# Two wide products and a sum for each rotation of the SSM, and one scan over two pairs

## The chip, the cores and the metric

The kernel runs on one core of a Trainium2 chip. The metric is the time of one execution on the device in microseconds. Five engines work side by side, each through its own queue in order: PE (matmuls), DVE (VectorE), ACT (ScalarE), POOL (GpSimd) and SP (here only transfers).

## The reference

One decoder block of 256 tokens and a model width of 2048, in float32. Cut to what the change touches:

```python
u    = rms_norm(x); proj = u @ w_in           # q, k, v, s_in, two gates
y_a  = diff_attention(q, k, v)                # 8 heads
a_bar = exp(lam * dt); b_bar = (a_bar - 1) / lam * b      # 64 groups x 64 complex states
bu   = einsum('gph,lgh->lgp', b_bar, s_in)
states = associative_scan(s[l] = a_bar * s[l-1] + bu[l])  # over the 256 tokens
y_s  = real(einsum('ghp,lgp->lgh', c, states)) + d * s_in
y_s  = gelu(y_s); y_s = y_s * sigmoid(y_s @ w_glu + b_glu)
merged = sigmoid(g_a) * (y_a @ w_attn_branch) + sigmoid(g_s) * (y_s @ w_ssm_branch)
x = x + rms_norm(merged @ w_out); x = x + rms_norm(swiglu(rms_norm(x)))
```

The decay of a state, a_bar = r * exp(i w), is taken apart: bu is turned back by the angle w * n of its token n, the two real parts are scanned with the real decay r alone, and the result is turned forward again. Each turn, a rotation, is four products and two sums.

## The kernel before

All matmuls of the main stream work in float32 by a split of each 128 x 1024 piece of weights into `hi` (ACT casts) and `lo` (DVE subtracts), from `do_split`. One k step of a block is four pairs of token half and column half with three matmuls of 512 columns each, 12 in all. The blocks follow one another: `ssm` (the projection of s_in), `q`, `k`, `v`, `ga0`, `ga1` (16 k steps each), `wa0`, `wa1` (8 each), `gs0`, `gs1` (16 each), then `glu`, which needs the output of the SSM, `ws0` and so on, and the feed-forward layer. `hi` and `lo` have three buffers each, so they run two to three k steps ahead of PE.

The rest is laid beside that stream as tasks, Python generators: `prep()` (decays, angles, the tables of sines and cosines, the input matrices), `u_parts()`, `ssm()` and `attn()`. After each k step `pump()` runs the first task on until the units that it yields exceed a budget: 1.2 units for a k step of block `ssm`, `SIDE` = 1.4 for the blocks up to `gs1`. Debt is carried over. `post_u` puts `u_parts()` first and appends `ssm()`; `post_v`, at the end of `v`, appends `attn()` and sets "switch", at which `ssm()` goes behind `attn()` in the list at its next pass. `glu_pre` calls `drain("s5")`: what is left of `ssm()` is then issued at once.

`pump` unpins the order: the program is handed to a planner (`schedule_with_timeline_sim=True`), which orders each engine's instructions while it builds the program, by a timeline of its own, and may take later ones forward when their inputs and buffers are ready. Tiles are given out from pools with a number of buffers: `side2` (the `bu` products of the SSM, the attention's scores) has one, `b8` six of 8 KB per partition.

`ssm()` works in 16 half steps (`hh`), two for each of 8 groups, of 128 partitions x 2 pairs x 256 tokens. In each:

- `table(hh + 1)` makes the next tables on POOL, six operations of 512 columns into `tcs` and `tss` (two buffers each, tags tabC and tabS);
- in odd half steps `group(g + 1)` prepares the output matrices (`cdup` on ACT, two transposes, `blkC`);
- the first rotation on DVE: four products of `bu` in PSUM with the tables into tA to tD (tags ssA to ssD), two sums;
- `finish` of the group before (8 matmuls and an operation on DVE), then the `bu` matmuls of the next half step (`bu_mm`) and the fetch of the one after;
- four scans of 256 columns, two for each pair;
- the second rotation: four products and two sums into `sre` and `sim`.

Yields in a half step: 1.2 three times, 0.7 twice, 1.2 twice, and 0.3 for `group`, 0.4 for `finish`.

Of the kernel before, what the change touches and what calls it, by code (L numbers as in the profile page):

```python
# [9 lines left out]
F32 = mybir.dt.float32  # L10
# [4 lines left out]
ALU = mybir.AluOpType  # L15
# [3 lines left out]
P = 128  # L19
S = 256  # L20
# [3 lines left out]
NG = 8  # L24
# [64 lines left out]
def hybrid_block_kernel(  # L89
# [9 lines left out]
    V, A, T = (InOrder(tc, e, pin) for e in (nc.vector, nc.scalar, nc.tensor))  # L99
    G = nc.gpsimd  # L100
# [17 lines left out]
    mixp = phase.enter_context(tc.tile_pool(name="mixp", bufs=1))  # L118
# [52 lines left out]
    ga = gap.tile([P, 2, 2, 1024], F32, name="ga")  # L171
# [229 lines left out]
    hold = {}  # L401
# [76 lines left out]
    def prep():  # L478
# [2 lines left out]
        G.affine_select(out=maskb, in_=maskb, pattern=[[-1, P]], compare_op=ALU.is_ge,  # L481
                        fill=-1e30, base=0, channel_multiplier=1)
        fl = lambda t_: t_.rearrange("p a b -> p (a b)")
        pp = Scratch([ga.rearrange("p a b c -> p (a b c)"), fl(small([P, 4, S], "sre")), fl(small([P, 4, S], "sim"))])
        braw = [big8(shape=(32, 2048)) for _ in range(2)]
        for ap, r, n in rows:
            G.dma_start(prow[r:r + n, :], ap)
# [38 lines left out]
        rr = mixp.tile([P, 32], F32, name="rr")  # L526
# [10 lines left out]
        fl = lambda t_: t_.rearrange("p a b -> p (a b)")  # L537
# [22 lines left out]
        for t_ in braw:  # L560
# [3 lines left out]
                          t_.rearrange("a (q h) -> a h q", h=16)[:, h, :], 32)  # L564
            bps.append(ps.rearrange("p (h a) -> p h a", h=16))
            yield 0.5
        bb = [mixp.tile([P, 32, 16], F32, name=nm("bb")) for _ in range(2)]
        bc = lambda c_: c_.unsqueeze(1).broadcast_to([P, 16, 32])
        tmp = [pp.tile([P, 16, 32], F32, name=nm("bt")) for _ in range(2)]
        for o, (c0, c1, op) in enumerate(((cre, cim, ALU.subtract), (cim, cre, ALU.add))):  # L570
# [6 lines left out]
        for base in (0, 4):  # L577
# [6 lines left out]
            for l in range(4):  # L584
                n = 1 << l
# [10 lines left out]
        hold.update(bb=bb, tabs=tabs, cn=cn)  # L596
        blkB, blkC = [], []
        for i in range(2):
            blkB.append([mixp.tile([P, 4, 32], F32, name=nm("blkB")) for _ in range(2)])
            blkC.append([mixp.tile([P, 4, 32], F32, name=nm("blkC")) for _ in range(2)])  # L600
            for t_ in blkB[i] + blkC[i]:
                G.memset(t_, 0.0)
        hold.update(blkC=blkC)
        yield 0.1
# [22 lines left out]
    def table(hh):  # L627
        (cb, sb), (ca, sa) = hold["tabs"]
        sl = slice(2 * hh, 2 * hh + 2)
        tcs = small([P, 2, 16, 16], "tabC", bufs=2)  # L630
        tss = small([P, 2, 16, 16], "tabS", bufs=2)
        t2 = small([P, 2, 16, 16], "tabt2")
        lo = lambda t_: t_[:, sl, :].unsqueeze(2).broadcast_to([P, 2, 16, 16])
        hi = lambda t_: t_[:, sl, :].unsqueeze(3).broadcast_to([P, 2, 16, 16])
        G.tensor_tensor(tcs, hi(ca), lo(cb), op=ALU.mult)
        G.tensor_tensor(t2, hi(sa), lo(sb), op=ALU.mult)
        G.tensor_tensor(tcs, tcs, t2, op=ALU.subtract)
        G.tensor_tensor(tss, hi(sa), lo(cb), op=ALU.mult)  # L638
        G.tensor_tensor(t2, hi(ca), lo(sb), op=ALU.mult)
        G.tensor_tensor(tss, tss, t2, op=ALU.add)  # L640
        r = lambda t_: t_.rearrange("p j a b -> p j (a b)")
        return r(tcs), r(tss)

    def u_parts():

# [22 lines left out]
    def ssm():  # L668
        uT = hold["yT"]
        nxt = table(0)  # L670

        def finish(g, bC, sre, sim):
            yp = side()
            for o, st in enumerate((sre, sim)):
                for j in range(4):
                    T.matmul(yp[32 * j:32 * j + 32, :S], bC[o][:, j, :], st[:, j, :],
                             start=(o == 0), stop=(o == 1), skip_group_check=True)
            V.scalar_tensor_tensor(uT[:, g, :], uT[:, g, :], dT[:, g:g + 1], yp[:, :S],
                                   op0=ALU.mult, op1=ALU.add)
# [37 lines left out]
        pend = None  # L717
        yield from group(0)
        fetch(0)
        bu = bu_mm(0)  # L720
        fetch(1)
        yield 1.0
        for hh in range(2 * NG):
            g, hf = hh // 2, hh % 2
            if hf == 0:
                bC = hold["bC"]
                sre = sim = None
            tcs, tss = nxt
# [4 lines left out]
            tA, tB, tC, tD = (small([P, 2, S], "ss" + n) for n in "ABCD")  # L733
            prr, pii = bu[:, :, 0:S], bu[:, :, S:2 * S]
            V.tensor_tensor(tA, prr, tcs, op=ALU.mult)
            V.tensor_tensor(tB, pii, tss, op=ALU.mult)
            yield 1.2
            V.tensor_tensor(tA, tA, tB, op=ALU.add)
            V.tensor_tensor(tC, pii, tcs, op=ALU.mult)
            yield 1.2  # L740
            V.tensor_tensor(tD, prr, tss, op=ALU.mult)
            V.tensor_tensor(tC, tC, tD, op=ALU.subtract)
            yield 1.2
            if pend:
                finish(*pend)
                pend = None
                yield 0.4
            if hold.pop("switch", None):
                yield "switch"
            if hh + 1 < 2 * NG:  # L750
                bu = bu_mm(1 - hf)
                if hh + 2 < 2 * NG:
                    fetch(hh + 2)
            for jj in range(2):
                rb = hold["rr"][:, 2 * hh + jj:2 * hh + jj + 1].broadcast_to([P, S])
                V.tensor_tensor_scan(tB[:, jj, :], rb, tA[:, jj, :], 0.0, op0=ALU.mult, op1=ALU.add)
                V.tensor_tensor_scan(tD[:, jj, :], rb, tC[:, jj, :], 0.0, op0=ALU.mult, op1=ALU.add)
                yield 0.7
            if sre is None:
                sre = small([P, 4, S], "sre")  # L760
                sim = small([P, 4, S], "sim")
            V.tensor_tensor(tA, tB, tcs, op=ALU.mult)
            V.tensor_tensor(tC, tD, tss, op=ALU.mult)
            V.tensor_tensor(sre[:, 2 * hf:2 * hf + 2, :], tA, tC, op=ALU.subtract)
            yield 1.2
            V.tensor_tensor(tB, tB, tss, op=ALU.mult)
            V.tensor_tensor(tD, tD, tcs, op=ALU.mult)
            V.tensor_tensor(sim[:, 2 * hf:2 * hf + 2, :], tB, tD, op=ALU.add)
            yield 1.2
            if hf == 1:  # L770
                pend = (g, bC, sre, sim)
        yield 2.5
        finish(*pend)
        y1h, y1l = big8(F32R, (P, 8, S)), big8(F32R, (P, 8, S))
# [185 lines left out]
    def first_load(k, r):  # L960
# [464 lines left out]
```

## Time and profile before

| | |
|---|---|
| median of 3 runs | 1436.42 us (1436.34 to 1437.39) |
| the profiled execution | 1436.86 us |
| its span, first to last instruction | 1435.1 us |
| busy: PE, DVE, ACT, POOL | 1375.7, 923.2, 680.8, 232.9 us |
| granted TensorE clock, mean | 0.985 |

The page gives busy times of the engines over the span and in 40 slices of 35.9 us (a digit is the busy share in tenths); the other views cut the trace by stretch, by group of instructions and by tile. In the names `side` is a tile in PSUM for side work, `acc` an accumulator of the main stream, `b` a tile of the pool `b8`. POOL's spans are rough, and matmuls are pipelined, so that their busy times overlap.

### The profile page before, as it was taken

How to read it: one execution, taken by the hardware profiler on the slowest of the kernel's cores; microseconds unless marked ns; L12 is line 12 of the kernel's file. 1: busy time of each engine (PE TensorE's matmuls, PEld its weight loads, DVE VectorE, ACT ScalarE, POOL GpSimd, SP SyncE). 2: the span in 40 equal slices, each digit the busy share in tenths (PEclk: the TensorE clock that was granted, in tenths of full speed). 3: DMA queues.
4: the chain of work that ended last, by engine and by line, in shares of the span. 5: the costliest groups of instructions: out<-in, count | busy, mean ns of one | idle time of the engine just before them, and what ended most of it. 6: DMA issues, size and time to landing. Idle time of an engine off the chain costs nothing.

```text
span 1435.1 us, 17346 instructions
## 1 busy us (share of the span) xinstructions
PE 1375.7 (96%) x6367; PEld 1115.7 (78%) x6367; DVE 923.2 (64%) x1122; ACT 680.8 (47%) x989; POOL 232.9 (16%) x195
## 2 busy tenths in 40 slices
PE   8998898999899879999999999999999999999997
PEld 6887676668676659888788888888888888888885
DVE  5965999967999975754764444444444445555555
ACT  4654443497443354444464444444444435444443
POOL 3293545500645500000000000000000000000001
PEclk9999999999999999999999999999999999999999
DMA  8688555444456465655576555556565564555651
GB/s 259 187 263 253 171 175 154 141 132 140 154 158 176 145 184 207 227 197 191 188 238 202 197 182 196 176 191 205 176 199 185 175 211 171 204 200 182 205 176 59
DMA packets 102006, 266.70 MB, mean 186 GB/s; under 512 B 10176, under 2 KB 17168, under 8 KB 98528
## 3 DMA queue, kind: packets, MB, share of 16 engines
q1 hardware_dynamic: 100704, 260.09, 56.1%
q10 hardware_dynamic: 608, 4.20, 0.8%
q0 software_dynamic: 608, 1.30, 0.4%
q8 instruction: 50, 0.82, 0.2%
q14 instruction: 36, 0.29, 0.1%
HBM read 257.16 MB, written 8.39 MB: 185 GB/s over the span
## 4 chain that ended last, share of the span: by engine, by line
issue 55%; PE 23%; DVE 15%; ACT 3%; DMA 2%; SPq 1%; POOL 0%; POOLq 0%; DVEq 0%; ACTq 0%
PE acc L41 22%; DVE lo L41 4%; DVE ssA L41 2%; DVE ssB L41 2%; DVE ssD L41 2%; PE side L41 2%; DVE ssC L41 2%; DMA raw<-in_w_in_dram 1%; DVE sim L41 1%; ACT hi L41 1%; SPq L623 1%; DMA raw<-in_w_glu_dram 1%; ACT prob L41 1%; DVE sre L41 1%; DVE b L41 1%
## 5 line engine op out<-in xcount | busy, mean ns | idle before, releaser
L41 DVE TENSOR_TENSOR lo<-raw,hi 128x1024 fp32r<-128x1024 f32 (+1 forms) x341 | 439.7, 1294 | 246.5 <-ACT hi L41 243.0
L41 ACT CAST hi<-raw 128x1024 fp32r<-128x1024 f32 (+1 forms) x340 | 355.0, 1051 | 399.0 <-PE acc L41 316.8
L41 PE MATMUL acc<-lo,zT_h 128*128 128x512 f32 x704 | 275.1, 391 | 0.0
L41 PE MATMUL acc<-hi,zT_l 128*128 128x512 f32 x704 | 274.3, 390 | 0.0
L41 PE MATMUL acc<-hi,zT_h 128*128 128x512 f32 x704 | 271.2, 393 | 0.2 <-ACT zT_h L41 0.2
L41 DVE TENSOR_TENSOR lo<-b,hi 128x1024 fp32r<-128x1024 f32 x124 | 151.1, 1224 | 147.6 <-ACT hi L41 147.6
L41 PE MATMUL acc<-lo,xT_h 128*128 128x512 f32 x512 | 207.4, 408 | 14.1 <-DVE lo L41 14.1
L41 PE MATMUL acc<-hi,xT_l 128*128 128x512 f32 x512 | 202.0, 397 | 0.0
L41 ACT CAST hi<-b 128x1024 fp32r<-128x1024 f32 x124 | 130.6, 1053 | 120.4 <-PE acc L41 104.0
L41 PE MATMUL acc<-hi,xT_h 128*128 128x512 f32 x512 | 165.8, 407 | 5.8 <-ACT hi L41 4.1
L41 PEld LDWEIGHTS acc<-hi,zT_h 128*128 128x128 f32 x704 | 132.3, 188 | 27.6 <-ACT zT_h L41 0.7
L41 PEld LDWEIGHTS acc<-hi,zT_l 128*128 128x128 f32 x704 | 132.3, 188 | 27.6
L41 PEld LDWEIGHTS acc<-lo,zT_h 128*128 128x128 f32 x704 | 132.3, 188 | 26.5
L41 PEld LDWEIGHTS acc<-lo,xT_h 128*128 128x128 f32 x512 | 98.8, 193 | 44.2 <-DVE lo L41 22.4
L41 PEld LDWEIGHTS acc<-hi,xT_h 128*128 128x128 f32 x512 | 97.6, 194 | 29.2 <-ACT hi L41 5.1
L41 PEld LDWEIGHTS acc<-hi,xT_l 128*128 128x128 f32 x512 | 98.3, 192 | 20.1 <-issue 0.8
L398 POOL TENSOR_TENSOR rstdf<-rstdfm,half 128x1 f32<-128x1 f32 x2 | 1.1, 546 | 691.6 <-DVE rstdfm L41 691.6
L41 PE MATMUL acc<-hi,b 128*128 128x512 f32 x256 | 84.1, 403 | 1.3 <-DVE ga L41 1.0
L638 POOL TENSOR_TENSOR tabS<-tabs,tabc 128x512 f32<-128x512 f32 x16 | 46.9, 2932 | 143.9 <-DVE ssB L41 143.9
L41 PE MATMUL acc<-lo,hTh 128*128 128x512 f32 x176 | 68.5, 389 | 0.0
L41 PE MATMUL side<-lo,hTh 128*128 128x512 f32 x176 | 68.5, 389 | 0.0
L41 PE MATMUL side<-hi,hTh 128*128 128x512 f32 x176 | 68.5, 389 | 0.0
(209 smaller groups left out, 1796.0 us busy)
## 6 DMA issues: line engine op xcount, KB each, us to landing
raw<-in_w_in_dram SPq DMA_DIRECT2D x127, 512.0 KB, 3.9
raw<-in_w_ffn_gate_dram SPq DMA_DIRECT2D x96, 256.0 KB, 2.8
raw<-in_w_ffn_up_dram SPq DMA_DIRECT2D x96, 256.0 KB, 3.1
raw<-in_w_ffn_down_dram SPq DMA_DIRECT2D x44, 512.0 KB, 3.7
b<-in_w_ffn_down_dram SPq DMA_DIRECT2D x22, 1024.0 KB, 4.9
b<-in_w_ffn_gate_dram SPq DMA_DIRECT2D x40, 512.0 KB, 3.8
b<-in_w_ffn_up_dram SPq DMA_DIRECT2D x40, 512.0 KB, 4.7
raw<-in_w_out_dram SPq DMA_DIRECT2D x32, 512.0 KB, 4.1
```

Of the source, the lines that this page charges most:

```text
L41: ins = f(*a, **kw)
L398: G.tensor_tensor(r, ms, half[:, :n], op=ALU.pow)
L623: nc.sync.dma_start(stack_b[:, j // 2, n, :, j % 2].rearrange("g q o n -> q g o n"), t_[32 * j:32 * j + 32])
L638: G.tensor_tensor(tss, hi(sa), lo(cb), op=ALU.mult)
```

## The change

The tables of a half step become one tile of three planes, minus sine, cosine and sine (`tab`); POOL makes the last two, ACT the first by `A.mul` with -1. A rotation is then a product of the real part with planes 0 and 1, one of the imaginary part with planes 1 and 2, each of 1024 columns with the part read twice by a broadcast, and a sum of 1024. The scans of both pairs are one of 512 columns for the real and one for the imaginary part; so that the second pair starts afresh, the decay is a tile of 512 columns with a zero at the start of each pair, which POOL fills for each half step (`decays`). `sre` and `sim` become one tile `st`, tA to tD become X and Y. `bb` and `blkB` move from their own tiles into one of the six buffers of `b8`. The yields become 1.3 three times, 1.2 twice, 1.3 three times.

```diff
-        bb = [mixp.tile([P, 32, 16], F32, name=nm("bb")) for _ in range(2)]
+        tmp8 = big8()
+        bb = [tmp8[:, 512 * i:512 * i + 512].rearrange("p (a h) -> p a h", a=32) for i in range(2)]
...
+        decay = mixp.tile([P, 2, S], F32, name="decay")
+        G.memset(decay[:, :, 0:1], 0.0)
...
     def table(hh):
-        tcs = small([P, 2, 16, 16], "tabC", bufs=2)
-        tss = small([P, 2, 16, 16], "tabS", bufs=2)
+        tab = small([P, 3, 2, S], "tab", bufs=2)
+        tcs, tss = (tab[:, i].rearrange("p j (a b) -> p j a b", a=16) for i in (1, 2))
...
+    def decays(hh):
+        d = hold["decay"]
+        G.tensor_copy(d[:, :, 1:S], hold["rr"][:, 2 * hh:2 * hh + 2].unsqueeze(2).broadcast_to([P, 2, S - 1]))
...
         nxt = table(0)
+        decays(0)
+        A.mul(nxt[:, 0], nxt[:, 2], -1.0)
...
-            V.tensor_tensor(tA, prr, tcs, op=ALU.mult)
-            V.tensor_tensor(tB, pii, tss, op=ALU.mult)
-            yield 1.2
-            V.tensor_tensor(tA, tA, tB, op=ALU.add)
-            V.tensor_tensor(tC, pii, tcs, op=ALU.mult)
-            yield 1.2
-            V.tensor_tensor(tD, prr, tss, op=ALU.mult)
-            V.tensor_tensor(tC, tC, tD, op=ALU.subtract)
-            yield 1.2
+            X, Y = (small([P, 2, 2, S], "ss" + n) for n in "XY")
+            both = lambda v: v.unsqueeze(1).broadcast_to([P, 2, 2, S])
+            V.tensor_tensor(X, both(bu[:, :, 0:S]), tab[:, 0:2], op=ALU.mult)
+            yield 1.3
+            V.tensor_tensor(Y, both(bu[:, :, S:2 * S]), tab[:, 1:3], op=ALU.mult)
+            yield 1.3
+            V.tensor_tensor(X, X, Y, op=ALU.add)
+            yield 1.3
...
-            for jj in range(2):
-                rb = hold["rr"][:, 2 * hh + jj:2 * hh + jj + 1].broadcast_to([P, S])
-                V.tensor_tensor_scan(tB[:, jj, :], rb, tA[:, jj, :], 0.0, op0=ALU.mult, op1=ALU.add)
-                V.tensor_tensor_scan(tD[:, jj, :], rb, tC[:, jj, :], 0.0, op0=ALU.mult, op1=ALU.add)
-                yield 0.7
...
+            for o in range(2):
+                V.tensor_tensor_scan(fl(Y[:, o]), fl(hold["decay"]), fl(X[:, o]), 0.0, op0=ALU.mult, op1=ALU.add)
+                yield 1.2
+            if hh + 1 < 2 * NG:
+                decays(hh + 1)
...
+            V.tensor_tensor(sh, both(Y[:, 1]), tab[:, 1:3], op=ALU.mult)
+            yield 1.3
+            V.tensor_tensor(X, both(Y[:, 0]), tab[:, 0:2], op=ALU.mult)
+            yield 1.3
+            if hh + 1 < 2 * NG:
+                A.mul(nxt[:, 0], nxt[:, 2], -1.0)
+            V.tensor_tensor(sh, sh, X, op=ALU.add)
+            yield 1.3
```

## Rows read from the trace of the kernel before

**Rows 1.** The page: the busy share of PE and DVE, 40 slices, in tenths.
```profile
PE   8998898999899879999999999999999999999997
...
DVE  5965999967999975754764444444444445555555
```
**Rows 2.** Table by stretches of instructions on tile acc alone (us; busy and count by engine).
```profile
251.00:345.60 94.60, 71.27 (x287) 51.97 (x285) 0.74 (x1) 2.04 (x3) 1.00 0.45 138
345.60:523.90 178.30, 149.05 (x598) 110.86 (x597) 5.88 (x9) 4.27 (x7) 0.98 0.53 161
```
**Rows 3.** The chain that ended last: a stretch of undisturbed matmuls (start us, us).
```profile
617.85 72.79 PE acc L41 x321
```
**Rows 4.** The table by stretches of all instructions: PE, PEld, DVE, ACT, POOL, clock.
```profile
140.50:251.00 110.50, 100.40 (x446) 76.71 (x445) 110.40 (x130) 46.86 (x64) 57.17 (x31) 0.95 0.56 169
251.00:345.60 94.60, 88.66 (x481) 67.87 (x480) 70.37 (x120) 64.22 (x161) 24.37 (x18) 1.00 0.45 138
345.60:523.90 178.30, 162.09 (x748) 121.81 (x746) 177.12 (x221) 81.30 (x126) 79.81 (x44) 0.98 0.53 161
```
**Rows 5.** Timelines of DVE, PE and ACT at the SSM's marks (start us, duration us).
```profile
251.07 0.68 DVE L41 TENSOR_TENSOR ssA<-side,tabC 128x512 f32<-128x512 f32 x1
...
345.61 0.64 PE L41 MATMUL side<-us,bs 96*128 96x256 f32 x4
...
519.89 0.68 DVE L41 TENSOR_TENSOR sim<-ssB,ssD 128x512 f32<-128x512 f32 x1
...
523.49 0.39 PE L41 MATMUL acc<-hi,xT_l 128*128 128x512 f32 x1
...
526.54 1.99 ACT L41 CAST hi<-raw 128x1024 fp32r<-128x1024 f32 x2 [5.85 <-DMA raw<-in_w_glu_dram]
...
532.24 0.80 PE L41 MATMUL acc<-b,hi 128*128 128x256 f32 x2 [8.37 <-ACT b L41]
```
**Rows 6.** Timeline of DVE late in gs1, POOL idle: starts and durations.
```profile
501.21 1.21 DVE L41 TENSOR_TENSOR lo<-raw,hi 128x1024 fp32r<-128x1024 f32 x1
502.34 0.68 DVE L41 TENSOR_TENSOR sre<-ssA,ssC 128x512 f32<-128x512 f32 x1
502.94 0.68 DVE L41 TENSOR_TENSOR ssD<-ssD,tabC 128x512 f32<-128x512 f32 x1
...
511.15 1.26 DVE L41 TENSOR_TENSOR_SCAN ssB<-rr,ssA 128x256 f32<-128x256 f32 x2
512.33 1.24 DVE L41 TENSOR_TENSOR_SCAN ssD<-rr,ssC 128x256 f32<-128x256 f32 x2
```
**Rows 7.** Groups of DVE instructions, 345.6 to 523.9 us: busy us, mean ns.
```profile
L41 DVE TENSOR_TENSOR lo<-raw,hi 128x1024 fp32r<-128x1024 f32 x50 | 70.1, 1408 | 0.0
L41 DVE TENSOR_TENSOR ssA<-ssA,ssB 128x512 f32<-128x512 f32 x9 | 10.0, 1116 | 0.0
L41 DVE TENSOR_TENSOR sim<-ssB,ssD 128x512 f32<-128x512 f32 x9 | 9.8, 1089 | 0.0
L41 DVE TENSOR_TENSOR ssC<-ssC,ssD 128x512 f32<-128x512 f32 x9 | 8.7, 967 | 0.0
L41 DVE TENSOR_TENSOR ssB<-side,tabS 128x512 f32<-128x512 f32 x9 | 6.1, 677 | 0.0
```
**Rows 8.** Groups over the whole span: a product with a broadcast operand.
```profile
L41 DVE TENSOR_TENSOR ga<-side,par 128x512 f32<-128x512 f32 x8 | 5.5, 687 | 3.7 <-PE side L41 3.7
```
**Rows 9.** Tile tabS and tabt: the shortest and longest table operations (min/median/max ns).
```profile
L639 POOL TENSOR_TENSOR tabt<-tabc,tabs x16: 1053/1061/2144, 108.3 to 488.9; 128x512 f32<-128x512 f32 x16
L638 POOL TENSOR_TENSOR tabS<-tabs,tabc x16: 1442/3178/4313, 102.8 to 482.0; 128x512 f32<-128x512 f32 x16
```
**Rows 10.** Tile qk: first and last start of the score matmuls, duration of a copy.
```profile
L41 PE MATMUL side<-qk x64: 272/374/379, 259.9 to 336.8; 64*128 64x128 f32 x32, 64*128 64x256 f32 x32
L41 ACT COPY qk<-side x8: 567/586/597, 231.6 to 330.2; 128x512 f32<-128x512 f32 x8
```
**Rows 11.** Tile cdup: first and last start of the copies.
```profile
L41 ACT COPY cdup<-cn x16: 292/299/311, 24.3 to 427.7; 128x128 f32<-128x128 f32 x16
```

More of the change, by code (lines that the diff above doesn't have):

```diff
@@ L483, in prep @@
         fl = lambda t_: t_.rearrange("p a b -> p (a b)")
-        pp = Scratch([ga.rearrange("p a b c -> p (a b c)"), fl(small([P, 4, S], "sre")), fl(small([P, 4, S], "sim"))])
+        pp = Scratch([ga.rearrange("p a b c -> p (a b c)"), small([P, 2 * 4 * S], "st")])
         braw = [big8(shape=(32, 2048)) for _ in range(2)]
@@ L598, in prep @@
         for i in range(2):
-            blkB.append([mixp.tile([P, 4, 32], F32, name=nm("blkB")) for _ in range(2)])
+            blkB.append([tmp8[:, c:c + 128].rearrange("p (a b) -> p a b", a=4)
+                         for c in (1024 + 256 * i, 1152 + 256 * i)])
             blkC.append([mixp.tile([P, 4, 32], F32, name=nm("blkC")) for _ in range(2)])
@@ L603, in prep @@
         hold.update(blkC=blkC)
+        decay = mixp.tile([P, 2, S], F32, name="decay")
+        G.memset(decay[:, :, 0:1], 0.0)
+        hold["decay"] = decay
         yield 0.1
@@ L640, in table @@
         G.tensor_tensor(tss, tss, t2, op=ALU.add)
-        r = lambda t_: t_.rearrange("p j a b -> p j (a b)")
-        return r(tcs), r(tss)
+        return tab
+    def decays(hh):
+        d = hold["decay"]
+        G.tensor_copy(d[:, :, 1:S], hold["rr"][:, 2 * hh:2 * hh + 2].unsqueeze(2).broadcast_to([P, 2, S - 1]))
     def u_parts():
@@ L670, in ssm, with finish @@
         nxt = table(0)
-        def finish(g, bC, sre, sim):
+        decays(0)
+        A.mul(nxt[:, 0], nxt[:, 2], -1.0)
+        def finish(g, bC, st):
             yp = side()
-            for o, st in enumerate((sre, sim)):
+            for o in range(2):
                 for j in range(4):
-                    T.matmul(yp[32 * j:32 * j + 32, :S], bC[o][:, j, :], st[:, j, :],
+                    T.matmul(yp[32 * j:32 * j + 32, :S], bC[o][:, j, :], st[:, o, j, :],
                              start=(o == 0), stop=(o == 1), skip_group_check=True)
@@ L726, in ssm @@
                 bC = hold["bC"]
-                sre = sim = None
-            tcs, tss = nxt
+                st = None
+            tab = nxt
             if hh + 1 < 2 * NG:
@@ L732, in ssm @@
                 yield from group(g + 1)
-            tA, tB, tC, tD = (small([P, 2, S], "ss" + n) for n in "ABCD")
-            prr, pii = bu[:, :, 0:S], bu[:, :, S:2 * S]
-            V.tensor_tensor(tA, prr, tcs, op=ALU.mult)
-            V.tensor_tensor(tB, pii, tss, op=ALU.mult)
-            yield 1.2
-            V.tensor_tensor(tA, tA, tB, op=ALU.add)
-            V.tensor_tensor(tC, pii, tcs, op=ALU.mult)
-            yield 1.2
-            V.tensor_tensor(tD, prr, tss, op=ALU.mult)
-            V.tensor_tensor(tC, tC, tD, op=ALU.subtract)
-            yield 1.2
+            X, Y = (small([P, 2, 2, S], "ss" + n) for n in "XY")
[6 more added lines that the diff above has]
+            yield 1.3
             if pend:
@@ L753, in ssm @@
                     fetch(hh + 2)
-            for jj in range(2):
-                rb = hold["rr"][:, 2 * hh + jj:2 * hh + jj + 1].broadcast_to([P, S])
-                V.tensor_tensor_scan(tB[:, jj, :], rb, tA[:, jj, :], 0.0, op0=ALU.mult, op1=ALU.add)
-                V.tensor_tensor_scan(tD[:, jj, :], rb, tC[:, jj, :], 0.0, op0=ALU.mult, op1=ALU.add)
-                yield 0.7
[L759 to L769, printed above, removed]
+            fl = lambda v: v.rearrange("p j n -> p (j n)")
+            for o in range(2):
+                V.tensor_tensor_scan(fl(Y[:, o]), fl(hold["decay"]), fl(X[:, o]), 0.0, op0=ALU.mult, op1=ALU.add)
+                yield 1.2
+            if hh + 1 < 2 * NG:
+                decays(hh + 1)
+            if st is None:
+                st = small([P, 2, 4, S], "st")
+            sh = st[:, :, 2 * hf:2 * hf + 2, :]
+            V.tensor_tensor(sh, both(Y[:, 1]), tab[:, 1:3], op=ALU.mult)
[6 more added lines that the diff above has]
+            yield 1.3
             if hf == 1:
-                pend = (g, bC, sre, sim)
+                pend = (g, bC, st)
         yield 2.5
```

## Prediction

> **What bounds the kernel now.** I read the page first. PE is nearly full in every slice but those between some 100 and 530 us, and there DVE is at its fullest [rows 1]. The time to be won or lost lies there: where PE is undisturbed, 321 accumulating matmuls take 72.79 us, 0.227 us each [rows 3]. I then cut the table by stretches at the SSM's own marks [rows 4]: the first six half steps of `ssm()` (140.5 to 251 us), the attention (to 345.6), the last nine half steps (to 523.9), the wait in front of `glu`. In the first DVE is busy for 110.4 of 110.5 us, in the third for 177.1 of 178.3: there DVE sets the pace and PE waits for `lo`. In the second DVE has 24 us to spare. At the end PE stands still for 8.4 us until the last gelu and cast are through [rows 5].
>
> A k step of the main stream (12 matmuls) needs 12 x 0.227 = 2.72 us of PE. The attention's stretch holds 287 of these matmuls, 24 k steps at 4.0 us, the third 598, 50 k steps at 3.6 [rows 2]: PE could do them in 2.72 each and the little work beside.
>
> **Part by part: the arithmetic on DVE.** Removed from each of 16 half steps: twelve products and sums of 512 columns and four scans of 256. Start to start an undisturbed 512 takes 0.60 us and a scan 0.59 (1.18 for two) [rows 6]: 12 x 0.60 + 4 x 0.59 = 9.56 us. Added: six of 1024 columns and two scans of 512. The 1024 columns of `lo` take 1.13 start to start [rows 6], so about 0.07 us per instruction is fixed. The new products read a broadcast operand and two of them PSUM; PSUM costs a product nothing now (677 ns [rows 7]), and a broadcast operand 687 [rows 8]. I take 1.13, and for a scan of 512 the two old ones less one fixed part, 1.11 (bounds 0.59 and 1.18). 6 x 1.13 + 2 x 1.11 = 9.0 us. Gain 0.55 us a half step, at most 8.8 us over 16.
>
> Beside POOL, DVE is slower: in the third stretch three of the four sums average 1116, 967 and 1089 ns against 677, 1.1 us a half step, and 50 `lo` average 1408 against 1210, another 1.1 [rows 6, 7]. POOL's six table operations (1.05 to 1.44 us at their shortest, up to 4.31 [rows 9]) stay and start at the same point, after the last read of the older table. POOL gets one more, the copy of the decays, for which the trace has no like: between 0.3 and 1.4 us. If a seventh operation disturbs as the six do, it costs DVE 0.4 us, if it falls on products from PSUM nothing; I take 0.25. Net gain on DVE: 0.3 us a half step, 5 us in all (bounds 2 and 8.8).
>
> `A.mul`, the minus sine plane, adds 16 ACT operations of 512 columns, 0.6 us each like `qk` (0.59 [rows 10]); ACT is busy for 81 of 178 us [rows 4], so I put it at nothing. But it waits for POOL in ACT's queue, with the `hi` casts and evacuations behind it; that is a rival below. `bb` and `blkB` in a `b8` buffer and the zeros of `decay` lie in `prep()`; I put them at nothing, since `u`'s buffer is free by then. Should the buffer be late, the first rotation (140.5 us) moves back with it, a few us.
>
> **Part by part: how the work is handed out.** This is the term that decides. A half step yields 7.4 units now (1.2 x 3 + 0.7 x 2 + 1.2 x 2) and 10.2 after (1.3 x 3 + 1.2 x 2 + 1.3 x 3), though it is no longer on DVE. Each k step of the main stream still releases 1.4. `prep()` and `u_parts()` need 37 units, of which the `ssm` block pays 16 x 1.2, so they end near k step 13 of `q`. From there to `glu` are 116 k steps, 162 units. Before, the attention (28.8), sixteen half steps (118), `group` and `finish` (5) and start and tail (8) ask for 160: it fits. After, they ask for 205. Followed k step by k step, twelve half steps and the thirteenth's scans are handed out in front of `glu`, and half steps 13, 14 and 15 (counted from 0) come only in `drain("s5")`, behind gs1's last matmul in program order, with nothing of the main stream beside them.
>
> Program order isn't the order that runs: the planner moves work forward. The `cdup` copy of the first group ran at 24.3 us, in the first block, though it is handed out in `q` [rows 11]. But a half step needs its `bu` matmuls on PE, and a planner that prefers what was handed out first puts them behind main matmuls whenever those are ready. Before, DVE is short and PE has holes; after, with 7.5 k steps to a half step instead of 5.5, the main stream is ahead of the SSM and has few. So I take it that in the third stretch the half steps come as they are handed out.
>
> **The sum, from the traced times.** Attention: its first scores ran at 259.9, after the seventh rotation (from 251.07) gave back the only `side2` buffer [rows 5, 10]. After, the "switch" falls one half step earlier, so six half steps precede it; it is handed out 5 k steps later than now (number 70 for 65, counted from the first block) but need not wait. I take the scores 12 us earlier, and 2 us from six faster half steps. From scores to the next rotation 345.6 - 259.9 = 85.7 us as now [rows 5, 10]: 331.6 us instead of 345.6.
>
> Those 14 us hold 3.5 of the attention's k steps, so that PE then has these more to do than the 598 matmuls of now: about 640. Now it needs some 158 us of its busy 162.1 there (598 x 0.227 = 136, and 150 side matmuls for 22; the rest are short gaps that a busy share hides); after, 158 + 42 x 0.227 - 3 (two half steps fewer at 1.4) = 165. DVE needs 53 x 1.13 for `lo`, 7 x 9.0, 7 x 2.5 beside POOL and 13 of other work, 154. PE is the longer: gs1 ends at 496.6 instead of 523.9.
>
> Then three half steps, from the rotation that starts 1.5 us before: 9.0 of DVE and about 3 us beside POOL, 12 each (bounds 9 and 14.6): 495.1 + 36 = 531, where the last sum ends now at 520.5 [rows 5]. From there to PE 11.7 us now; two `hi` casts waited for a transfer in front of the last gelu [rows 5], which will be long done: 10. `glu` starts at 541 instead of 532.2, 9 us late, and nothing behind it changes. The traced execution took 1436.86 us (span 1435.1 and 1.8 around it), the median of the three runs is 1436.42: 1436.4 + 9 = 1445.
>
> **The rivals.** *DVE stays the limit to the end* (chance 0.35). The planner does fill holes, the half steps come as DVE is free, and no tail is left. Then the total DVE work decides: minus 2 to 8.8 us, and 1.7 from the tail's transfer, 1426 to 1435, likeliest 1431. For it: 177.1 of 178.3 us busy now [rows 4], the early `cdup` [rows 11]. Against it: 43 units more than are released. The point from which it decides: if the `bu` matmuls of the last three half steps run before PE's last gs1 matmul. One or two of them moved forward leave it near 1436 to 1440.
>
> *Tables and products exclude one another in the tail* (0.1). If each waits out the other's whole instruction, 6.8 us of DVE with two SBUF operands and some 7.9 of POOL add up, less nothing but what POOL does under the 2.3 us of products from PSUM: 14.6 a half step, and 1453. The rows show less, 2.2 us lost for 11.4 of POOL [rows 4, 7]. [...]
>
> *ACT waits for POOL* (0.1). Each `A.mul` sits in ACT's order where the planner thinks the table done; the chip's POOL takes up to 4.31 us for one operation [rows 9]. `hi` has some 3 us to spare (two k steps of 2.72, less 1.05 and 1.3 for `hi` and `lo`); 1 us lost in each of 15 gives 1460.
>
> **How the numbers follow.** The tail as summed has 0.45 (1439 to 1451), the two worse cases 0.2 (1453 and 1460), the first rival 0.35 (1426 to 1440 with its mixed form). About 0.2%, 2.9 us, is what a measurement of this kernel tells from no change. The rival splits into 0.24 below 1433.5 and 0.11 within; of the tail 0.04 falls within. So faster 0.24, same 0.15, slower 0.61. The range, 1427 to 1459, leaves 0.1 on either side.
>
> **What would show it.** Right: first scores near 246 us, gs1's last matmul near 497, then PE idle for over 40 us with three half steps of long products alone on DVE, POOL busy throughout. A 1024 product at 1.2 us busy and a scan of 512 at 1.2 confirm the prices. Wrong: the last rotation before gs1's end and a wait in front of `glu` no longer than the 8.4 us of now; DVE idle in the last nine half steps waiting for POOL; ACT's `hi` behind POOL.

## The result and the profile after

The changed kernel takes 1448.84 us (median of 4 runs, 1448.68 to 1450.59) for 1436.81 of the kernel before (4 runs): a ratio of 1.0086, 95% interval 1.0069 to 1.0104. Its profiled execution took 1448.94 us with a span of 1447.2; everything behind the start of `glu` is as long as before (903.2 us for 902.9).

So the whole difference has been made when `glu` starts, at 544.0 us for 532.2. That start can be taken apart into three terms: the start of the first rotation, DVE's busy time from there to `glu`, and its idle time in between. Two rows of the table by stretches, first of the kernel before and then of the one after, from the first rotation to `glu` (behind the bounds and the length: PE, PEld, DVE, ACT, POOL, each busy us and count; clock; DMA share; GB/s):

```profile
140.50:532.20 391.70, 351.15 (x1673) 266.39 (x1671) 362.09 (x476) 198.01 (x358) 161.34 (x91) 0.97 0.52 158
```
```profile
147.00:544.00 397.00, 352.79 (x1674) 270.50 (x1672) 354.69 (x345) 208.55 (x374) 186.54 (x106) 0.97 0.53 158
```

The first rotation is 6.5 us later, DVE is busy for 7.4 us less, and it is idle for 42.3 us instead of 29.6, 12.7 more: 6.5 - 7.4 + 12.7 = 11.8. Both stretches hold 108 `lo`. Counted from one start to the next, the 7.4 us are, but for rounding, 3.2 from the SSM's own instructions (175.0 us before, 171.8 after), 3.3 from the attention's and the evacuations', and 1.5 from short subtractions behind the last gelu, which lie in front of `glu`'s first matmul before and behind it after; `lo` takes 0.5 more. So less than half of it is the new arithmetic.

Where the idle time lies shows the same table at the marks of [rows 4]:

```profile
147.00:239.70 92.70, 82.01 (x373) 62.40 (x371) 92.15 (x69) 41.23 (x60) 56.82 (x32) 0.98 0.57 168
239.70:339.40 99.70, 95.95 (x494) 75.04 (x495) 69.78 (x114) 68.32 (x164) 22.93 (x16) 0.98 0.47 140
339.40:531.40 192.00, 172.84 (x795) 132.46 (x794) 183.85 (x155) 89.69 (x137) 106.80 (x59) 0.97 0.53 161
```

One half step fewer stands in front of the attention (six). In the attention DVE is idle for 29.9 us where it was for 24.2, behind it for 8.2 where it was for 1.2. The clock is not the cause: 0.98, 0.98 and 0.97 here, 0.95, 1.00 and 0.98 there.

The prices, from the groups of DVE's instructions from the first rotation behind the attention to the last sum (busy us, mean ns):

```profile
L41 DVE TENSOR_TENSOR lo<-raw,hi 128x1024 fp32r<-128x1024 f32 x54 | 77.2, 1437 | 5.8 <-ACT hi L41 5.8
L41 DVE TENSOR_TENSOR_SCAN ssY<-decay,ssX 128x512 f32<-128x512 f32 x20 | 23.4, 1205 | 0.0
L41 DVE TENSOR_TENSOR ssX<-ssX,ssY 128x1024 f32<-128x1024 f32 x10 | 18.1, 1808 | 0.0
L41 DVE TENSOR_TENSOR st<-st,ssX 128x1024 f32<-128x1024 f32 x10 | 17.2, 1716 | 0.0
L41 DVE TENSOR_TENSOR ssY<-side,tab 128x1024 f32<-128x1024 f32 x10 | 12.1, 1209 | 0.0
```

A product from PSUM takes 1209 ns, a scan 1205, as forecast. The sums, both of whose operands lie in SBUF, take 1808 and 1716, and the two products of the rotation back, whose operands lie there too, 1407 and 1297.

The late first rotation is ACT's (e2 below takes it away). ACT's timeline before it, and the group of its waits for POOL (us in total, times, longest):

```profile
101.21 0.51 ACT L41 COPY b<-b 64x64 f32<-64x64 f32 x2
109.59 0.63 ACT L41 ACTIVATE tab<-tab 128x512 f32<-128x512 f32 x1 [7.87 <-POOL tab L645]
110.12 1.98 ACT L41 CAST hi<-raw 128x1024 fp32r<-128x1024 f32 x2
```
```profile
ACT tab L41 <- POOL tab L645: 68.5, 15, 9.1
```

ACT stands at the first `A.mul` for 7.87 us until POOL has made the table, with two `hi` casts behind it in its queue. In all, 15 of the 16 `A.mul` wait, 68.5 us together.

At the end there is no long drain. DVE's last rotation and last sum, then PE from the last `bu` matmuls on:

```profile
522.52 1.21 DVE L41 TENSOR_TENSOR ssX<-side,tab 128x1024 f32<-128x1024 f32 x1
...
535.10 1.22 DVE L41 TENSOR_TENSOR st<-st,ssX 128x1024 f32<-128x1024 f32 x1
```
```profile
508.77 0.64 PE L41 MATMUL side<-us,bs 96*128 96x256 f32 x4
...
531.05 0.39 PE L41 MATMUL acc<-hi,xT_l 128*128 128x512 f32 x1
536.38 1.92 PE L41 MATMUL side<-st,blkC 128*32 128x256 f32 x12 [4.93 <-DVE st L41]
543.97 1.43 PE L41 MATMUL acc<-b,hi 128*128 128x256 f32 x5 [5.67 <-ACT b L41]
```

The last rotation starts before gs1's last matmul (531.05). PE then stands still for 4.93 us for the last sum and 5.67 for the last gelu and casts, where it stood still once for 8.37 before [rows 5].

### The profile page after: what moved, and what is told of

It reads as the page before. It is cut to its first block, busy times and chain, and to the rows that moved or that the text cites. A ratio compares the mean times of both kernels' runs of the same rounds, so it can differ in the third digit from the quotient of the medians.

```text
span 1447.2 us, 17280 instructions
## 1 busy us (share of the span) xinstructions
PE 1377.5 (95%) x6367; PEld 1119.7 (77%) x6367; DVE 914.5 (63%) x994; ACT 691.3 (48%) x1007; POOL 254.8 (18%) x212
## 4 chain that ended last, share of the span: by engine, by line
issue 53%; PE 20%; DVE 10%; POOL 2%; ACT 2%; DVEq 0%; POOLq 0%; ACTq 0%
PE acc L41 18%; DVE ssX L41 3%; DVE ssY L41 3%; DVE st L41 2%; PE side L41 2%; DVE lo L41 2%; ACT hi L41 1%; DVE b L41 0%; POOL tab L642 0%; POOL tab L645 0%; ACT L41 0%; POOL decay L651 0%; DVE ga L41 0%; POOL tab L643 0%; POOL tabt L644 0%
## 5 line engine op out<-in xcount | busy, mean ns | idle before, releaser
L41 ACT CAST hi<-raw 128x1024 fp32r<-128x1024 f32 (+1 forms) x340 | 354.5, 1050 | 357.7 <-PE acc L41 275.7
L41 PE MATMUL acc<-hi,xT_h 128*128 128x512 f32 x512 | 165.5, 409 | 16.8 <-ACT hi L41 12.7
L41 PE MATMUL acc<-lo,hTh 128*128 128x512 f32 x176 | 68.5, 389 | 0.0
L41 PE MATMUL side<-hi,hTh 128*128 128x512 f32 x176 | 68.5, 389 | 0.0
L41 PE MATMUL side<-lo,hTh 128*128 128x512 f32 x176 | 68.5, 389 | 0.0
L41 PE MATMUL acc<-hi,hTh 128*128 128x512 f32 x176 | 68.3, 390 | 0.0
```

The source lines that it names most:

```text
L41: ins = f(*a, **kw)
```

## The experiments

Three suspects stood at the start: the slower hand-out (10.2 units for a half step instead of 7.4), `A.mul` in ACT's queue, and the decays. Each was taken back alone, and the hand-out alone put into the kernel before. Each row of the table by stretches below runs from the first rotation to `glu`; the three terms of all of them stand in one table behind the experiments. The letters of the theories are explained in the expectations.

**The hand-out of before in the changed kernel** (e1): yields of 1.2 three times, 0.7 twice, 0.8 three times, 7.4 in all.

```diff
-            yield 1.3
+            yield 1.2
...
-                yield 1.2
+                yield 0.7
...
-            yield 1.3
+            yield 0.8
```

> The changed kernel with the units of the kernel before: a half step yields 7.4 (1.2 three times, 0.7 twice, 0.8 three times) instead of 10.2; nothing else. If the slower handing out costs the time (theory P), seven half steps again precede the attention, the last one is handed out in front of glu, and it takes 1437 to 1441 us. If the negation that waits for POOL in ACT's queue costs it (theory A), or POOL's decay copies beside DVE (theory D), it stays at 1447 to 1451, with the first rotation at 147 us as in the changed kernel.

Measured: 1437.32 us, ratio 0.9997 (0.9989 to 1.0006).

```profile
147.00:533.00 386.00, 352.66 (x1673) 270.50 (x1672) 353.01 (x345) 199.95 (x367) 181.82 (x106) 0.97 0.51 157
```

The first rotation stays at 147.0, DVE is as busy (353.0), but idle for 33.0 us instead of 42.3: the whole loss is gone, 9.3 us of it as idle time, and the 6.5 at the start are still in. PE goes from gs1 to `glu` without a gap.

**The minus plane made by POOL** (e2), at both places.

```diff
-                A.mul(nxt[:, 0], nxt[:, 2], -1.0)
+                G.tensor_scalar(nxt[:, 0], nxt[:, 2], -1.0, None, op0=ALU.mult)
...
```

> The changed kernel with the minus sine plane made by POOL right behind the sine, instead of by ACT. Theory A: no hi cast waits for a table any more, the first rotation comes back from 147 to about 140.5 us, and 6 to 10 us are won: 1439 to 1443. Theory P: 1447 to 1451, as the order of the half steps is what it was. Theory D: slower by 2 to 5 us, 1451 to 1454, since POOL has an eighth operation in each half step.

Measured: 1448.09 us, 1.0076 (1.0062 to 1.0090).

```profile
141.10:544.60 403.50, 354.09 (x1674) 270.58 (x1672) 363.04 (x345) 202.26 (x360) 206.57 (x120) 0.96 0.51 156
```

The 5.9 us at the start are won, and DVE's busy time rises by 8.3 with not one instruction more: POOL has eight operations for each half step beside it instead of seven. The scans take most of it, 1428 ns on average instead of 1205, 7.1 us for the 32 of them. The stall was real and its removal worth nothing, since it was paid for in another term.

**The scans of before** (e3): four of 256 columns with a broadcast decay, no copies of the decays.

```diff
-        decays(0)
...
-                V.tensor_tensor_scan(fl(Y[:, o]), fl(hold["decay"]), fl(X[:, o]), 0.0, op0=ALU.mult, op1=ALU.add)
+                for jj in range(2):
+                    rb = hold["rr"][:, 2 * hh + jj:2 * hh + jj + 1].broadcast_to([P, S])
+                    V.tensor_tensor_scan(Y[:, o, jj], rb, X[:, o, jj], 0.0, op0=ALU.mult, op1=ALU.add)
...
-            if hh + 1 < 2 * NG:
-                decays(hh + 1)
```

> The changed kernel with the scans of before: four of 256 columns with the decay as a broadcast column, no decay copies on POOL (their zeros stay). Theory D: lo and the wide sums get shorter (1.41 to some 1.34 us for lo, 2.0 to some 1.7 for the sums), 1 us a half step less 0.1 for two more scans, 1437 to 1444. Theories P and A: 1446 to 1451.

Measured: 1444.45 us, 1.0055 (1.0042 to 1.0068).

```profile
147.80:541.10 393.30, 353.96 (x1673) 270.14 (x1671) 350.84 (x376) 206.85 (x374) 166.10 (x91) 0.96 0.51 159
```

Four scans instead of two and yet 3.9 us less of DVE: the wide scan loses more through its POOL copy than it wins. The saving isn't where it was expected: `lo` averages 1430 ns instead of 1406, and it is the rotation back that got shorter, its sum from 1850 to 1426, its products from 1439 and 1291 to 1215 and 1214.

**The slow hand-out in the kernel before** (e4): the old arithmetic with yields of 1.3 three times, 1.2 twice, 1.95 twice, 10.2 in all.

```diff
-            yield 1.2
+            yield 1.3
...
-                yield 0.7
+                yield 1.2
...
-            yield 1.2
+            yield 1.95
```

> The kernel before with the units of the change: 10.2 a half step (1.3 three times, 1.2 twice, 1.95 twice), the arithmetic untouched. Theory P: it loses what the change lost, 1443 to 1450 against 1436.4. Theories A and D: as before, 1434 to 1438.

Measured: 1434.09 us, 0.9980 (0.9972 to 0.9989).

```profile
141.10:529.90 388.80, 348.28 (x1673) 265.75 (x1671) 356.80 (x473) 202.37 (x360) 160.28 (x91) 0.97 0.52 160
```

The theory that the hand-out alone costs 9 to 12 us falls: here it gains 2.7. Idle time rises by 2.4 us, busy time falls by 5.3; 1.5 of these are the short subtractions that now lie behind the end of the stretch, the other instructions are the same. What the slow hand-out costs has to be something that it does to the new arithmetic.

**Both small costs away, at either hand-out** (e5, e6): the edits of e2 and e3 together, then also that of e1. What is left of the change is the wide products and sums.

> The changed kernel at its own slow hand-out (10.2 units), with the four scans of 256 of before and with the minus plane made by POOL instead of ACT: what is left of the change is the wide products and sums and the slow hand-out. Removing the minus plane from ACT alone gave 0.7 us, removing the decays alone 4.4. Theory S (small costs that add up: ACT behind POOL at the start, the decays beside DVE, a coarser hand-out): the two together give at least their sum, 1440 to 1443, and more if each had hidden the other. Theory T (the first product of the rotation back writes `st` itself, so all three of its operations, 4.5 us, wait for a late `finish`, where before only the last sum of each half, 1.3 us, did; and at the slow hand-out `finish` of the third group comes only after the attention): the stretch from the first rotation after the attention to the next stays near 33 us, and the time stays at 1443 or above. Theory C (a DVE whose instructions are 1.2 to 2 us long serves `lo` too late): 1443 or above, and so in the kernel without a plane too.

> The same with the hand-out of before (7.4 units). The changed kernel with this hand-out alone took 1437.3, 6.5 us of which it lost at the start behind POOL, and DVE set its pace after that. Theory S: both costs are gone, 1428 to 1432. Theory T: `finish` is not late at this hand-out, so as S. Theory C: no gain from removing either, 1435 to 1438, PE waiting for `lo` as now.

Measured: e5 1440.08 us, 1.0025 (1.0016 to 1.0035); e6 1423.93 us, 0.9913 (0.9899 to 0.9926). First e5, then e6:

```profile
141.00:536.80 395.80, 353.18 (x1673) 269.16 (x1671) 357.08 (x376) 201.19 (x360) 188.68 (x105) 0.97 0.53 158
```
```profile
140.90:521.10 380.20, 349.79 (x1674) 268.84 (x1673) 353.12 (x376) 192.45 (x352) 186.70 (x105) 0.98 0.54 160
```

e6 beats both kernels: the first rotation where it was before, 9.0 us less of DVE (the SSM's own instructions 7.2 less; four `lo` fewer lie in front of `glu`), 2.5 us less of idle time, and no gap in PE in front of `glu` (its last matmul of gs1 ran at 520.83). The gain expected was too small: it was added up from gains at the slow hand-out, where the decays were worth 4.4 us (e3); at the old one they are worth 8.5 (e9, below). At the slow hand-out (e5) 16 us of it are lost, 11.6 of them idle time; its time is what theory S said, its stretch behind the attention (33.1 us, below) what theory T said.

**No third plane** (e7, e8): products over two planes only, in one tile of four in which the work runs in place; sums and differences of 512 columns; the scans of before. `st` is written only by the last sum and difference. e7 at the slow hand-out, e8 at the old one.

```diff
-            V.tensor_tensor(X, X, Y, op=ALU.add)
+            V.tensor_tensor(W[:, 0], W[:, 0], W[:, 3], op=ALU.add)
+            V.tensor_tensor(W[:, 2], W[:, 2], W[:, 1], op=ALU.subtract)
...
-            V.tensor_tensor(sh, both(Y[:, 1]), tab[:, 1:3], op=ALU.mult)
...
+            V.tensor_tensor(W[:, 0:4:2], both(W[:, 1]), tab, op=ALU.mult)
+            V.tensor_tensor(W[:, 1:4:2], both(W[:, 3]), tab, op=ALU.mult)
...
+            V.tensor_tensor(sh[:, 0], W[:, 0], W[:, 3], op=ALU.subtract)
+            V.tensor_tensor(sh[:, 1], W[:, 2], W[:, 1], op=ALU.add)
```

> Slow hand-out (10.2 units), wide products over a table of two planes only, in one tile of four planes in which the scans and the products back run in place; the sums and differences are again of 512 columns (four instead of two of 1024), the scans of 256 are those of before, and no minus plane is made by anyone. `st` is written only by the last sum and difference. DVE work without POOL 4 x 1.13 + 4 x 0.60 + 4 x 0.59 = 9.28 us a half step for 9.56 of before. Theory S: near the kernel of before at the slow hand-out (1434.1), less at most 0.28 x 16: 1430 to 1434. Theory T: the same, and the stretch from the first rotation after the attention to the next about 30 us. Theory C: 1441 or above.

> The same at the hand-out of before (7.4 units). Theories S and T: DVE sets the pace in both stretches and has 0.28 us less a half step: 1432 to 1436, the last sum at 516 to 519 us instead of 519.9. Theory C: 1437 to 1441.

Measured: e7 1433.45 us, 0.9979 (0.9970 to 0.9987); e8 1432.09 us, 0.9970 (0.9960 to 0.9980). First e7, then e8:

```profile
138.40:527.30 388.90, 348.28 (x1674) 265.93 (x1672) 356.15 (x409) 201.66 (x360) 149.53 (x91) 0.97 0.54 160
```
```profile
139.50:526.70 387.20, 348.85 (x1673) 268.45 (x1671) 358.25 (x411) 194.94 (x355) 147.67 (x91) 0.98 0.53 159
```

Here the hand-out matters for 1.4 us only, which the intervals don't tell from nothing (e8's last sum, at 514.1, came 2 us earlier than expected). So products of 1024 columns on DVE are no cause by themselves; the long sums, which e7 and e8 don't have, are in e6, the fastest of all, and theory C falls with it. e5 and e7 differ by 5.9 us of idle time at the same hand-out, and more than half of that (6.2 us for 2.7) lies in one place, the half step behind the attention. DVE there after the change, with the first matmuls of `finish` on PE, then DVE in e7:

```profile
340.13 1.23 DVE L41 TENSOR_TENSOR ssX<-side,tab 128x1024 f32<-128x1024 f32 x1 [0.81 <-PE side L41]
...
346.66 2.34 DVE L41 TENSOR_TENSOR_SCAN ssY<-decay,ssX 128x512 f32<-128x512 f32 x2
...
365.25 0.64 PE L41 MATMUL side<-st,blkC 128*32 128x256 f32 x8
...
367.87 1.22 DVE L41 TENSOR_TENSOR st<-ssY,tab 128x1024 f32<-128x1024 f32 x1
...
369.34 2.03 DVE L41 TENSOR_TENSOR st<-st,ssX 128x1024 f32<-128x1024 f32 x1
...
373.30 1.21 DVE L41 TENSOR_TENSOR ssX<-side,tab 128x1024 f32<-128x1024 f32 x1
```
```profile
354.20 0.69 DVE L41 TENSOR_TENSOR st<-ssW 128x512 f32<-128x512 f32 x1
...
355.14 0.68 DVE L41 TENSOR_TENSOR st<-ssW 128x512 f32<-128x512 f32 x1
355.85 1.22 DVE L41 TENSOR_TENSOR ssW<-side,tab 128x1024 f32<-128x1024 f32 x1
```

The scans are done at 349, but `st` has one buffer, and `finish` of the third group, its last reader, runs on PE only at 365.3. In e7, where `finish` runs at 351.6, the two short sums alone wait for it; after the change the product that writes `st` itself does too (367.87), and the sum behind it. From this rotation to the next it is 33.2 us after the change and 33.1 in e5, but 30.0 in e7 and 30.1 in e4. At the old hand-out seven half steps precede the attention, and this `finish` is through at 238 us.

**The same, in the changed kernel alone** (e12): the products back go into X and, in place, into Y, and only the sum writes `st`.

```diff
-            V.tensor_tensor(sh, both(Y[:, 1]), tab[:, 1:3], op=ALU.mult)
+            V.tensor_tensor(X, both(Y[:, 0]), tab[:, 0:2], op=ALU.mult)
...
-            V.tensor_tensor(X, both(Y[:, 0]), tab[:, 0:2], op=ALU.mult)
+            V.tensor_tensor(Y, both(Y[:, 1]), tab[:, 1:3], op=ALU.mult)
...
-            V.tensor_tensor(sh, sh, X, op=ALU.add)
+            V.tensor_tensor(sh, Y, X, op=ALU.add)
```

> The changed kernel as it is (10.2 units, minus plane on ACT, decays), but the two products back go into X and, in place, into Y, and only the sum writes `st`; one edit, no more or fewer instructions. Theory T (in the half step behind the attention the product that writes `st` and the sum behind it, 3.2 us, wait for `finish`, where only the sums did before): that stretch, 33.2 us after and 30.1 in the old arithmetic at the same hand-out, becomes 30 to 31.5; DVE's idle time from there to the last sum, 7.5 us, falls by 2 to 4; 1444.5 to 1447. If the wait isn't on the path: stretch 30 to 33, the last sum at 534 to 537 as now, 1448 to 1450.

Measured: 1445.29 us, 1.0062 (1.0048 to 1.0075).

```profile
146.00:540.10 394.10, 351.61 (x1674) 268.22 (x1672) 353.77 (x345) 208.13 (x374) 182.33 (x106) 0.96 0.53 159
```

The time is 3.5 us down, within what theory T said, the stretch is 31.6 us (336.0 to 367.5), at the upper end of it, and idle time behind the attention falls by 2.8. The rest isn't as clean: the planner's order changed ahead of the attention too, where 5 us of idle time came in, and as much went in the attention.

**`finish` handed out earlier** (e11): the same wait from the other side.

```diff
+            if pend:
+                finish(*pend)
+                pend = None
+                yield 0.4
             X, Y = (small([P, 2, 2, S], "ss" + n) for n in "XY")
...
-            if pend:
-                finish(*pend)
-                pend = None
-                yield 0.4
```

> The changed kernel as it is (10.2 units throughout), but `finish` of the last group is handed out ahead of the next half step's first product instead of behind its sum. Theory T (the first half step behind the attention stands still since its first product back writes `st`, which the late `finish` still reads): `finish` of the third group some 8 to 11 us earlier, the stretch from the first rotation behind the attention to the next 24 to 29 us instead of 33.2, DVE's idle time there 7.5 less 3 to 5, 1443 to 1446. If that wait is only one of several that end at the same time (PE's order, the attention's own work): stretch 32 to 34 us, 1447 to 1449.

Measured: 1449.22 us, 1.0084 (1.0071 to 1.0097).

```profile
144.90:544.80 399.90, 356.33 (x1674) 272.92 (x1672) 357.47 (x345) 208.24 (x374) 182.71 (x106) 0.96 0.52 158
```

Nothing, and no test: `finish` ran at 363.5 us, at k step 99 as in the changed kernel, e4, e5 and e7. Handing a task out earlier doesn't run it earlier when the planner has another reason to hold it; which one (a buffer for `side`, or the attention's order) stays open.

**Seven half steps at the old hand-out, nine at the slow one** (e10): the yields of e1 while `hh` is under 7, then those of the change.

```diff
-            yield 1.3
+            yield 1.2 if hh < 7 else 1.3
...
```

> The changed kernel with the hand-out of before (7.4 units) for the first seven half steps and its own (10.2) for the last nine. Theory H (the loss is made at the attention: six half steps stand in front of it instead of seven, DVE waits 31 us in it instead of 25, then for `finish` in the half step behind it, and one half step more is left for the end): seven half steps first, scores at 264, first rotation after the attention at 348 as in the run with the old hand-out, the last sum at 521 to 525, 1437 to 1441. Theory L (the loss is made by handing the last half steps out late): scores and first rotation as under H, but the last three rotations late, the last sum at 530 or more, DVE idle over 8 us behind the attention, 1444 to 1449.

Measured: 1444.64 us, 1.0050 (1.0037 to 1.0063).

```profile
147.00:540.00 393.00, 354.05 (x1673) 270.29 (x1671) 353.94 (x344) 205.07 (x371) 184.42 (x106) 0.97 0.53 157
```

Both theories hold a part: the scores (262.8), the first rotation behind the attention (348.2) and the last sum (524.5) come where theory H had them, the time where theory L had it. With the attention in its old place 4.2 of the 11.5 us between e1 and the changed kernel are won; the other 7.3 come with the slow hand-out of the last nine. PE at the end, first here, then in e1:

```profile
533.34 0.62 PE L41 MATMUL side<-st,blkC 128*32 128x256 f32 x2
540.02 1.22 PE L41 MATMUL acc<-b,hi 128*128 128x256 f32 x4 [6.05 <-ACT b L41]
```
```profile
524.37 1.06 PE L41 MATMUL side<-st,blkC 128*32 128x256 f32 x12
```

The last `finish`, the gelu, its table loads and the casts take 6.7 us up to `glu` here and 7.6 after the change. At the old hand-out they run beside gs1's last matmuls (up to 532.8) and cost nothing; at the slow one PE waits for them.

**The decays kept, at the old hand-out** (e9): the edits of e1 and e2.

> The changed kernel at the hand-out of before (7.4 units) with the minus plane made by POOL, the decays and the scans of 512 kept: between the run with the old hand-out alone (1437.3) and the one that also has the old scans (1423.9) it takes the ACT waits away and leaves the decays. Start of glu = first rotation + DVE's busy time from there + its idle time: 147.0 + 353.0 + 32.9 = 533 with ACT, 140.9 + 353.1 + 27.0 = 521 without both. Theory A (the gain of 13 us was ACT's waiting alone): first rotation 141, busy 353, idle 27, 1423 to 1427. Theory D (an eighth POOL operation slows DVE as much as the waits cost; at the slow hand-out busy rose from 354.7 to 363.0 when the minus plane went to POOL): first rotation 141, busy 360 to 363, idle 27 to 30, 1431 to 1436.

Measured: 1432.38 us, 0.9961 (0.9947 to 0.9975). The profile is of the shortest of its six runs (1428.25), with a first rotation some 4 us earlier than elsewhere:

```profile
136.50:524.70 388.20, 351.11 (x1674) 268.53 (x1673) 357.66 (x345) 193.58 (x354) 204.28 (x120) 0.98 0.52 156
```

Of the 13.4 us between e1 and e6, 4.9 go with `A.mul` off ACT (some 6 at the start and 2.5 of idle time, less 4.7 of DVE's time beside POOL's eighth operation) and 8.5 with the decays (6.9 by the ratios; e9's runs spread from 1428 to 1436). Theory A, that the waits were everything, falls.

The three terms of all kernels (us; worked out from the rows above, each of one profiled execution):

| | median | first rotation | DVE busy | DVE idle |
|---|---|---|---|---|
| before | 1436.8 | 140.5 | 362.1 | 29.6 |
| after | 1448.8 | 147.0 | 354.7 | 42.3 |
| e1 old hand-out | 1437.3 | 147.0 | 353.0 | 33.0 |
| e2 minus plane on POOL | 1448.1 | 141.1 | 363.0 | 40.5 |
| e3 old scans | 1444.5 | 147.8 | 350.8 | 42.5 |
| e4 before, slow | 1434.1 | 141.1 | 356.8 | 32.0 |
| e5 wide only, slow | 1440.1 | 141.0 | 357.1 | 38.7 |
| e6 wide only, old hand-out | 1423.9 | 140.9 | 353.1 | 27.1 |
| e7 no plane, slow | 1433.5 | 138.4 | 356.2 | 32.8 |
| e8 no plane, old hand-out | 1432.1 | 139.5 | 358.3 | 29.0 |
| e9 = e1 + e2 | 1432.4 | 136.5 | 357.7 | 30.5 |
| e10 slow after seven | 1444.6 | 147.0 | 353.9 | 39.1 |
| e11 `finish` early | 1449.2 | 144.9 | 357.5 | 42.4 |
| e12 sum into `st` | 1445.3 | 146.0 | 353.8 | 40.3 |

As the stretches end with `glu`, they don't hold quite the same work. Those of e1 and e9 have 105 `lo`, that of e6 has 104, those of e8 and e10 have 107 and the rest 108, some 1.3 us each; the short subtractions behind the last gelu, 1.5 us, lie inside it before and in e1, e6, e8 and e9. A few us of DVE busy can so fall in front of `glu` in one row and behind it in another. Where `A.mul` isn't on ACT, the first rotation came between 138.4 and 141.1 us, and in e9 at 136.5.

## Why the prediction was right or wrong

The time (1445 forecast, 1448.8 measured) and the sign were right, and the mechanism that was to give them wasn't there. It is a hit by errors that cancel.

- **The arithmetic on DVE: right.** 1.13 for 1024 columns and 1.11 for the scan stood against 1.13 to 1.14 and 1.13 start to start; the net gain of 5 us (2 to 8.8) against 2.7, which is 3.2 from the SSM's instructions less 0.5 for `lo`: inside the bounds, near the lower one. The rest of the 7.4 is other work. The copy of the decays was put at 0.25 us of DVE a half step, and at 0.3 to 1.4 us of POOL, which no row showed: it took 1.52 us in the median of 16, 0.61 at its shortest. e3 returned 3.9 us while it added 16 x 0.1 for the four scans: some 0.34 each.
- **`A.mul` put at nothing: wrong.** Its rival had the right mechanism and place in the queue, and the wrong price. It was not 1 us in each half step: 68.5 us of waits cost 6.5 at the first table, and elsewhere little that the other terms don't already hold. The trace of before could have given the first one: the fifth of the first table's six operations started at 108.3 us [rows 9], and by that start a `hi` that waits for the sixth comes some 7 us late (an estimate; in the changed kernel ACT waited 7.87 us). K step 32 (of 12 main matmuls each, counted from the first block) started at 119.2 us instead of 112.7. `bb` and `blkB` in a `b8` buffer cost 0.6 us at most: with `A.mul` off ACT the first rotation is at 141.1 us (e2) for 140.5.
- **Six half steps before the attention, scores near 246: right** (244.5).
- **"From scores to the next rotation 85.7 us as now": wrong.** It took 95.6, where it was 86.4 (the 85.7 end at the `bu` matmuls in front of the rotation). The next half step started at k step 91.1 or 91.2 in every run that was slow from the start, and the scores came at k step 65.8: 25.3 k steps lie between, where there were 21.1. The table by stretches on tile acc alone, from the first scores to the next rotation, first before and then after:

```profile
259.90:346.30 86.40, 63.53 (x255) 46.30 (x254) 0.74 (x1) 2.04 (x3) 1.00 0.45 135
```
```profile
244.50:340.10 95.60, 74.68 (x305) 55.70 (x305) 0.75 (x1) 2.07 (x3) 1.00 0.48 143
```

With its side work PE is busy for 92.0 of the 95.6 us and was for 80.5 of the 86.4, so most of what the 50 matmuls more need is added to the stretch. The step that failed took a span of time where the hand-out fixes the k step at which the stretch ends.

- **"In the third stretch the half steps come as they are handed out", gs1's end at 496.6, a drain of 36 us: wrong.** The `bu` matmuls of the last three half steps ran at 471.7, 490.7 and 508.8, ahead of PE's last gs1 matmul at 531.05, and PE's wait in front of `glu` was 10.6 us in two parts instead of over 40. By the prediction's own deciding point this was the rival "DVE stays the limit to the end". Its mechanism came true, DVE busy for 183.85 of 192 us behind the attention.
- **That rival's 1431: wrong by 18 us**, since it took only DVE's total work and the tail's transfer into account. What it left out is the start, 6.5, and 12.7 of idle time. The idle time is 5.7 more in the attention and 7 behind it, 3 of these in the half step whose `st` waited for `finish` (shown by e7 and e12); for the other 4 no run isolates the cause, and some 2.5 of them are there at the old hand-out too (e1, from the attention to the last sum: 3.3 us idle for 0.8).
- **The hand-out "is the term that decides": right for the changed kernel (e1), wrong as a rule.** It decides with the wide arithmetic, 11.5 us in the change and 16 in e5 for e6, and gains 2.7 in the old arithmetic (e4). It costs where something in the half step is late as well, as `st` is here (e12); that this is the whole reason isn't shown, and how much of the 16 is the order ahead of the attention isn't settled.
- **Tables and products exclude one another in the tail: no case**, since POOL's last operation in front of `glu` ended at 517.0 us and the last rotation started at 522.5. In the body they did, with 2.03 to 2.08 us for instructions of 1.1, more wholly than the prediction read from its rows (below).

## What to carry to other kernels

Write the start of the stage that has to wait as a sum, first start + busy + idle of the engine that sets the pace, and ask of each edit which of the three it changes: here the busy time fell by 7.4 us, 6.5 were lost at the start and 12.7 as idle time. Look as well at which instructions the stretch holds: of the 7.4 the new arithmetic's own were 3.2. An operation put on another engine to save the busy one still had a place in that engine's queue here (`A.mul`: 68.5 us of ACT's waits, 6.5 us at the start) or took turns with the busy one (the decays: 3.9 us of DVE's busy time, e3), and an output buffer should be written by the last instruction that can write it, so that a late reader stops that one alone (3.5 us, e12). The wide products and sums alone, with the minus plane on POOL and the hand-out and scans of before, are 0.9% faster than the kernel before (e6).

## What the runs showed of the hardware

POOL and DVE took turns by whole instructions. The timelines of POOL and of DVE after the change, in the half step of above:

```profile
369.23 1.06 POOL L640 TENSOR_TENSOR tab<-tabc,tabc 128x512 f32<-128x512 f32 x1 [6.56 <-DVE st L41]
370.25 2.04 POOL L643 TENSOR_TENSOR tab<-tabs,tabc 128x512 f32<-128x512 f32 x1
372.25 2.28 POOL L642 TENSOR_TENSOR tab<-tab,tabt 128x512 f32<-128x512 f32 x1
374.61 1.06 POOL L644 TENSOR_TENSOR tabt<-tabc,tabs 128x512 f32<-128x512 f32 x1
```
```profile
371.30 2.08 DVE L41 TENSOR_TENSOR lo<-raw,hi 128x1024 fp32r<-128x1024 f32 x1
373.30 1.21 DVE L41 TENSOR_TENSOR ssX<-side,tab 128x1024 f32<-128x1024 f32 x1
374.43 1.21 DVE L41 TENSOR_TENSOR ssY<-side,tab 128x1024 f32<-128x1024 f32 x1
```

The sum at 369.34 took 2.03 us: some 0.9 for the rest of POOL's first operation, then its own 1.13. POOL's second, 1.06 alone, lasted 2.04, until 1 us after that sum; `lo`, 1.13 alone, ended 1 us after POOL's second. The products from PSUM at 373.30 and 374.43 kept their 1.21, and POOL its 1.06 beside them. From the means of [rows 7] the prediction read a smaller loss; they are means over instructions that met POOL and such that didn't: of the 50 `lo` there, 36 took 1.19 to 1.22 us and 14 took 1.48 to 2.31. The three instructions that met in the lines above, of 1.1 us each alone, took 2.03, 2.04 and 2.08 us.

Added POOL operations were therefore not free although POOL was busy for only 186.5 of 397 us after the change: the minus plane on POOL cost DVE 8.3 us (e2), 4.7 (e9 for e1) and 6.2 (e5 for e3), 0.3 to 0.5 us for each of the 16.

The scans went by their columns: 1.13 us start to start for 512 (the two at 346.66), where two of 256 took 1.18, and a product of 512 0.60 [rows 6]. The wider scan so saved 0.05 us of 1.18.
